# A hybrid attention/retention layer: merged rows reloaded in place by thirds, first rows of x kept on chip, weights loaded in quarters, and a scheduler that models the DMA queue

## The chip, the cores and the metric

The kernel runs on one core of one Trainium2 chip. The metric is the device time of one execution in microseconds (us). The core's engines run side by side, each through its own list of instructions: TensorE (PE) multiplies matrices, VectorE (DVE), ScalarE (ACT) and GpSimd (POOL) work elementwise, and SyncE (SP) issues all DMAs, among them the DMA transposes, in the order of its list.

## The reference, cut to what matters

One step of a single layer, for 1024 prompt rows and 32 sample rows (T = 1056), model width 1024, 8 heads:

```python
h   = RMSNorm(x)
z   = h @ w_in          # q/k/v of differential attention, q/k/v/gate of retention, two branch gates
o_a = DiffAttn(h)       # chunk-block-causal, two softmax maps per head: a = p0 - lam * p1
o_r = Retention(h)      # per-frame causal, decay, rotary, chunkwise-recurrent
x   = x + (sigmoid(g_a) * o_a + sigmoid(g_r) * o_r) @ w_o
x   = x + SwiGLU(RMSNorm(x))
x   = x + sigmoid(RMSNorm(x) @ w_ple_gate) * (p @ w_ple)
```

The new keys, values and retention states are outputs too.

## The kernel before

Every large matrix product is done as three fp16 products of high and low parts (mm3, L520; project, L860 to L862): for one step over 128 of the inner width there are three matmuls.

**The heads (0 to about 965 us).** The rows of x are normalised, transposed by PE (t, L834) and kept as xh (high and low part, 1056 rows). For each of 8 heads and 9 row blocks (eight of 128 rows, the ninth the sample) there is a unit A and a unit B. Unit A projects q, k, v and the retention q and k: 24 matmuls of 128x512 into a PSUM tile pj. Then come the scores sc (L1003 to L1006), the row maximum nm (DVE, L1013), its scaled negative nb (L1015), the exponential p (ACT, L1023), the difference of the two softmax maps and its split into fp16 parts (DVE), a DMA transpose aT<-p (SP, L1056), and the product po with v (L1064 to L1068). Unit B, which follows four units later (LAG), projects the retention v and the gates and computes the retention: a transposition on PE (pr, L1257), its copy qT (L435), pr and por (L1270 to L1273), the mask inn (DVE, L1276), por again (L1278). The merged result ms of a unit is transposed by DMA to mixT (L1357) and stored to DRAM (mix_d, by the helper store, L423 to L432, so that its line is L427). q and kT reach their layout by DMA transposes too (L1193, L1195).

Weights come as blocks of 1 MB (load_block_steps, L439): a stage buffer st is filled, an absolute maximum or a sum of squares gives a scale, and the block is split into fp16 parts. The very first blocks come as four quarters of 256 KB, each with its own DMA (due == 0, L449 on), the others in one DMA (L454).

**w_o.** When a head's blocks are in mix_d, last_mix (L1455 on) loads the merged rows back as mixs, by row ranges of 352 and by high and low part (L1463). mixs is a new tile of the pool of xh, allocated after the last projection. wo_rows multiplies the first 352 rows (block 0) by w_o, with the matching rows of x loaded as xr (L1417), adds, and stores them to x1_d. For the other blocks (1 of 352 rows, 2 and 3 of 176) w_o follows in the next stage; residual(0) reads block 0 back from x1_d (L1706) and scales it for the feed-forward.

**The rest (from about 998 us).** Residuals and norms of the four blocks (L1687 sums of squares, L1719 to L1728 scaling on DVE), the gate and up products as seven Strassen-like products over combined inputs (tT, x parts; parts are combined on DVE at L1595 on, weights at L549 to L558), the down projection, and the gated embedding at the end.

**What sets the order.** Each piece of work is a Python generator. A list scheduler (class Flow, L112) simulates the engines M (PE), V, S, G and D (the DMA issues): every step names an engine and a cost, the earliest possible one is taken, and instructions are emitted in that order. PE, DVE, ACT and POOL run their lists in exactly that order. Buffers are counted (get and put), events order the rest (wait and set). SP's list is written in the order in which the DMAs are emitted. Costs are plain functions: V, S, G for the elementwise engines, DM(mb) for a load (2.9 us per MB), X(us) and xbar(tiles) for stores and transposes, and fixed delays for the landing.

Of the kernel before, what the change touches and what calls it, by code (L numbers as in the profile page):

```python
# [11 lines left out]
F32 = mybir.dt.float32  # L12
# [9 lines left out]
P = 128  # L22
# [5 lines left out]
NT = 9  # L28
# [15 lines left out]
LAG = 4  # L44
NQ = 6
# [41 lines left out]
def DM(mb):  # L87
    return {"D": mb * 2.9}


def X(us):
    return {"D": us}


def xbar(tiles):

    return 1.15 + 0.006 * tiles


def landed(tiles):  # L100

    return ("delay", 1.3 + 0.02 * tiles)
# [9 lines left out]
class Flow:  # L112
    def __init__(self, buffers, shared=False):
        self.shared = shared
        self.free = {e: 0.0 for e in "MVSGD"}
        self.port = {"V": 0.0, "G": 0.0}
        self.buffers = {k: [0.0] * n for k, n in buffers.items()}
# [4 lines left out]
    def add(self, gen, prio=0, at=None):  # L122
        self.n += 1
        self._step([gen, prio, self.n, self.now if at is None else at, None, False], None)

    def _step(self, c, value):

        while True:
# [43 lines left out]
            elif kind == "delay":  # L172
                c[3] += key
            elif kind == "wait":
# [5 lines left out]
    def run(self):  # L180
        while self.ready:
# [12 lines left out]
            if isinstance(us, Own):  # L194
                self.port[e] = start + us
            c[3] = start + us + (0.0 if e == "M" else LAT)
# [19 lines left out]
def kernel(  # L216
# [63 lines left out]
    acc0 = const.tile([P, CH], F32, name="acc0")  # L280

# [43 lines left out]
    def weight_scale(amax, n, gi, tag, pool=True, norm=False, total=False, at_bank=None):  # L325
# [29 lines left out]
        d = sm(n, tag + "d", 6)  # L355
# [67 lines left out]
    def store(out, in_, key, us, event=None):  # L423

        yield ("delay", us)
        yield X(0.5)
# [3 lines left out]
        if key:  # L430
            yield ("delay", 2.5)
            yield ("put", key)  # L432
# [6 lines left out]
    def load_block_steps(src, w, b, gi, tag, rowf, out, tail=False, due=None, late=None, hold=None):  # L439
# [4 lines left out]
        if due == 0:  # L444
# [6 lines left out]
            yield ("set", "wl%d" % b)  # L451
        else:
            yield DM(1.0)
            nc.sync.dma_start(out=st, in_=src)  # L454
            yield ("delay", 3.0)
# [105 lines left out]
    def load_gu(j):  # L561

        yield ("get", "st")
        st = stage()[:, 0:KD * 256].rearrange("p (k u c) -> p k u c", k=KD, u=2)
        yield DM(1.0)
        nc.sync.dma_start(out=st, in_=wgu[j])
        yield ("delay", 2.0)
# [40 lines left out]
        yield ("put", "st")  # L608


    with ExitStack() as pa:
# [3 lines left out]
        id16 = ca.tile([P, P], F16, name="id16")  # L615
# [50 lines left out]
        def const_a():  # L666
# [3 lines left out]
            yield ("delay", 2.0)  # L670
# [14 lines left out]
        def const_c():  # L685
# [3 lines left out]
            yield ("delay", 2.0)  # L689
            yield ("set", "id")  # L690
            yield ("wait", ("x", 0))
            yield V(P)
            nc.vector.tensor_copy(id16, id32)

        def const_g():
# [3 lines left out]
            yield ("delay", 2.0)  # L699
# [12 lines left out]
        def const_b():  # L712
# [11 lines left out]
            yield ("delay", 2.0)  # L724
# [69 lines left out]
        def norm_x(i):  # L794
# [15 lines left out]
            yield ("delay", 3.0)  # L810
# [80 lines left out]
        def rms_small(ss, R, n, tag):  # L891

            yield GP(0, 0.5 + 0.2 * n)
# [5 lines left out]
        def prep_head_a(h, w, e):  # L899
# [8 lines left out]
            yield X(0.5)  # L908
            nc.sync.dma_start(out=s0[0:64], in_=st0[h])
            gr = hp.tile([P, P], F32, tag="grn", name="grn", bufs=2)  # L910
            yield X(0.5)
# [9 lines left out]
        def cache_steps(h, dA, e):  # L921
# [5 lines left out]
            for dst, src in ((kc[0:64], ckT[h]), (kc[64:128], ckT[h]), (vc, cv[h])):  # L927
                yield X(0.9)
                nc.sync.dma_start(out=dst, in_=src)
            yield ("delay", 4.0)  # L930
# [61 lines left out]
        def attend(key, i, R, q4, sblocks, masked, vblocks, NK, sc_ap, do_ap):  # L992
# [3 lines left out]
            for ms in ((0, 1),) if NK <= 512 else ((0,), (1,)):  # L996
# [19 lines left out]
                for m in ms:  # L1016
                    yield ("get", "p")
                    yield S(NK, 0.14)
# [36 lines left out]
            yield X(xbar(2 * nb_ * R // 16))  # L1055
# [1146 lines left out]
```

## Time and profile before

| What | us |
|---|---|
| Median of three runs | 1839.96 (1838.93 to 1841.03) |
| The profiled execution | 1841.03 |
| Its span | 1839.2 |
| PE busy | 1791.3 |
| DVE busy | 1456.2 |
| ACT busy | 1064.7 |
| POOL busy | 613.6 |

The profile is of one execution. A row of its timeline holds start, length, engine, line of the kernel, operation, output<-inputs by the program's names, and in brackets the idle time before it and what ended that. A row of its list of waits gives who waited for whom, the total, the number of times and the longest. A row of its DMA list gives the size of one DMA in KB and the median time from issue to landing.

### The profile page before, as it was taken

What the parts mean: (1) busy time and instruction counts of PE and PEld (TensorE: products, weight loads), DVE (VectorE), ACT (ScalarE), POOL (GpSimd) and SP (SyncE); (2) the same over time, 40 slices, a digit from 0 to 9 for tenths busy, and PEclk for the clock granted to TensorE, in tenths of its full rate; (3) what the DMA queues carried; (4) which work ended last, traced back from release to release, by engine and by line L of the source; (5) the groups of instructions that cost most, each with busy time, mean ns of one, the idle gap of its engine ahead of it and who ended that gap; (6) DMA issues with size and microseconds to landing.
All of it is one profiled execution on the core that took longest, in us unless ns stands there. A gap on an engine that the chain in (4) does not pass through costs nothing.

```text
span 1839.2 us, 37083 instructions
## 1 busy us (share of the span) xinstructions
PE 1791.3 (97%) x13391; PEld 1153.4 (63%) x13391; DVE 1456.2 (79%) x3883; ACT 1064.7 (58%) x2750; POOL 613.6 (33%) x1036
## 2 busy tenths in 40 slices
PE   7899999999999999999989999999999999999999
PEld 3455555555555555555556867777777766666666
DVE  7888788788787887888885889999999967544553
ACT  7677777677777777777654445655556522102421
POOL 3554546454554555545530002323232100000110
PEclk9999999999999999999999999999999999999999
DMA  6344434345443543435367203221211163221111
GB/s 202 106 124 110 111 82 100 99 107 125 87 116 91 119 111 83 123 80 126 84 151 252 78 5 105 82 93 59 70 47 63 40 264 107 67 78 47 51 48 44
DMA packets 235563, 180.98 MB, mean 98 GB/s; under 512 B 187345, under 2 KB 217553, under 8 KB 227186
## 3 DMA queue, kind: packets, MB, share of 16 engines
q1 hardware_dynamic: 235378, 178.61, 34.6%
q8 instruction: 105, 1.72, 0.4%
q14 instruction: 80, 0.66, 0.1%
HBM read 112.34 MB, written 27.02 MB: 76 GB/s over the span
## 4 chain that ended last, share of the span: by engine, by line
PE 82%; DVE 10%; DMA 3%; ACT 2%; issue 2%; POOL 2%; SPq 0%; POOLq 0%; ACTq 0%; DVEq 0%
PE pj L860 10%; PE pj L861 10%; PE pj L862 9%; PE ps L521 9%; PE ps L522 9%; PE ps L523 9%; PE ps L1571 4%; PE ps L1570 4%; PE ps L1569 4%; DMA aT<-p 2%; PE sc L1003 2%; PE sc L1006 2%; PE pj L871 1%; PE po L1064 1%; PE po L1068 1%
## 5 line engine op out<-in xcount | busy, mean ns | idle before, releaser
L860 PE MATMUL pj<-w,xh 128*128 128x512 f16 x1024 | 389.9, 381 | 3.1 <-ACT w L512 1.7
L861 PE MATMUL pj<-w,xh 128*128 128x512 f16 x1024 | 390.0, 381 | 0.8 <-DVE w L514 0.8
L862 PE MATMUL pj<-w,xh 128*128 128x512 f16 x1024 | 389.9, 381 | 0.0
L521 PE MATMUL ps<-mixs,w 128*128 128x176 f16 (+1 forms) x864 | 231.2, 273 | 2.0 <-DVE xr L1432 1.7
L523 PE MATMUL ps<-mixs,w 128*128 128x176 f16 (+1 forms) x864 | 231.3, 273 | 1.4 <-DVE w L549 1.4
L522 PE MATMUL ps<-mixs,w 128*128 128x176 f16 (+1 forms) x864 | 231.2, 273 | 0.9 <-DVE mixs L1595 0.9
L523 PEld LDWEIGHTS <-w 128*128 128x128 f16 x1632 | 160.0, 98 | 53.8 <-issue 5.4
L522 PEld LDWEIGHTS <-w 128*128 128x128 f16 x1632 | 160.0, 98 | 48.5 <-issue 2.1
L521 PEld LDWEIGHTS <-w 128*128 128x128 f16 x1632 | 160.2, 98 | 48.2 <-issue 0.9
L862 PEld LDWEIGHTS <-xh 128*128 128x128 f16 x1024 | 100.4, 98 | 123.2 <-issue 3.2
L860 PEld LDWEIGHTS <-xh 128*128 128x128 f16 x1024 | 101.0, 99 | 89.2 <-issue 2.2
L861 PEld LDWEIGHTS <-xh 128*128 128x128 f16 x1024 | 100.4, 98 | 85.2 <-issue 3.7
L558 POOL TENSOR_TENSOR st<-st 128x512 f32<-128x512 f32 x54 | 71.8, 1330 | 237.6 <-DVE w L549 182.6
L522 PE MATMUL ps<-tT,w 128*128 128x352 f16 (+1 forms) x504 | 137.3, 277 | 3.2 <-DVE tT L1595 3.2
L523 PE MATMUL ps<-tT,w 128*128 128x352 f16 (+1 forms) x504 | 137.3, 277 | 0.0
L521 PE MATMUL ps<-tT,w 128*128 128x352 f16 (+1 forms) x504 | 137.3, 277 | 0.0
L1023 ACT ACTIVATE p<-sc,nb,scs 128x256 f32<-128x256 f32 (+7 forms) x128 | 106.2, 831 | 51.1 <-DVE nb L1015 37.9
L549 DVE SCALAR_TENSOR_TENSOR w<-st,gus,w 128x512 f16<-128x512 f32 x126 | 128.4, 1022 | 0.0
L1013 DVE TENSOR_REDUCE nm<-sc 128x1 f32<-128x640 f32 (+6 forms) x112 | 102.7, 917 | 23.0 <-PE sc L1006 22.0
L1571 PE MATMUL ps<-a,w 128*128 128x352 f16 x312 | 97.5, 313 | 0.5 <-DVE w L1776 0.5
L1570 PE MATMUL ps<-a,w 128*128 128x352 f16 x312 | 97.5, 313 | 0.0
L1569 PE MATMUL ps<-a,w 128*128 128x352 f16 x312 | 97.5, 312 | 0.0
(442 smaller groups left out, 4707.5 us busy)
## 6 DMA issues: line engine op xcount, KB each, us to landing
st<-in_win_dram SPq DMA_DIRECT2D x30, 1024.0 KB, 5.3
st<-in_wgu_dram SPq DMA_DIRECT2D x22, 1024.0 KB, 4.9
st<-in_wdn_dram SPq DMA_DIRECT2D x16, 704.0 KB, 4.1
out_dram<-kv SPq DMA_DIRECT2D x64, 128.0 KB, 1.9
a_d<-a SPq DMA_DIRECT2D x9, 528.0 KB, 2.7
b<-a_d SPq DMA_DIRECT2D x9, 528.0 KB, 7.1
mixs<-mix_d SPq DMA_DIRECT2D x6, 704.0 KB, 7.2
x<-x_d SPq DMA_DIRECT2D x8, 528.0 KB, 7.7
```

The lines of the kernel that those rows point to most:

```text
L521: nc.tensor.matmul(out=ps, lhsT=wh, rhs=ah, start=first, stop=False)
L522: nc.tensor.matmul(out=ps, lhsT=wh, rhs=al, start=False, stop=False)
L523: nc.tensor.matmul(out=ps, lhsT=wl, rhs=ah, start=False, stop=last)
L549: nc.vector.scalar_tensor_tensor(out=w[:, i, 1], in0=src, scalar=s, in1=w[:, i, 0], op0=ALU.mult, op1=ALU.subtract)
L860: nc.tensor.matmul(out=ps, lhsT=xhi, rhs=w[:, k, 0], start=(k == 0), stop=False)
L861: nc.tensor.matmul(out=ps, lhsT=xhi, rhs=w[:, k, 1], start=False, stop=False)
L862: nc.tensor.matmul(out=ps, lhsT=xh[:, k, 1, t0:t0 + P], rhs=w[:, k, 0], start=False, stop=(k == KD - 1))
L1013: nc.vector.tensor_reduce(out=nm[0:R, mc], in_=pv, axis=AX.X, op=ALU.max, negate=True)
L1023: nc.scalar.activation(pt[0:R, 0:NK], ps[0:R, p0:p0 + NK], AF.Exp, bias=nb[0:R, m:m + 1], scale=sc_ap[0:R], accum_out=Z[0:R, m:m + 1])
L1569: nc.tensor.matmul(out=ps, lhsT=wt[:, 0, j], rhs=a[:, 0, cs], start=(first and j == js[0]), stop=False)
L1570: nc.tensor.matmul(out=ps, lhsT=wt[:, 1, j], rhs=a[:, 0, cs], start=False, stop=False)
L1571: nc.tensor.matmul(out=ps, lhsT=wt[:, 2, j], rhs=a[:, 1, cs], start=False, stop=(last and j == js[-1]))
```

## The change

Merged rows. They are now loaded into xh itself. last_mix starts when the last head begins its fifth block; each third waits until the last head's B projections no longer read its rows (event free), and then is loaded (L1484 of the new file). The first product with w_o waits for the first third through the event mc, 5.5 us in the scheduler's time.

Block 0. xrow_load loads the first 352 rows of x before their use, six of the eight row groups into a weight stage buffer (st) and two into a tile of their own, x67. wo_rows adds into them, they stay there, and residual(0) and the combinations read them in place; the reload from x1_d is gone, the store to it stays. The stage buffer is given back by rows_free; until then the next stage has one stage buffer, and the second gate/up load has a tile of its own, sx.

Weights. Every block loaded by load_block_steps comes as four DMAs of 256 KB.

Scheduler. A DMA step now carries its size. Flow keeps a time at which the queue is free, adds the size by 0.26 MB per us (0.2 for a transpose), and lets landed() wait for that time. Some costs are changed, and the projection order is written as a string (ORDER) that begins with four A units, as the lag did. The transposed-merge buffers are 3 instead of 4, and an unused fp16 identity goes.

```diff
-def DM(mb):
-    return {"D": mb * 2.9}
-
-
-def X(us):
-    return {"D": us}
+class Dma(float):
+    mb, turn = 0.0, False
+
+
+def DM(mb, turn=False):
+    d = Dma(1.15 + 1.5 * mb if turn else 0.4)
+    d.mb, d.turn = mb, turn
+    return {"D": d}
...
+            if isinstance(us, Dma):
+                self.queue = max(self.queue, start + (0.9 if us.turn else 0.5)) + us.mb / (0.2 if us.turn else 0.26)
+                c[6] = max(c[6], self.queue + (1.3 if us.turn else 1.05))
+                c[3] = start + us
...
-            yield DM(1.0)
-            nc.sync.dma_start(out=st, in_=src)
-            yield ("delay", 3.0)
+            for q in range(4):
+                yield DM(0.25)
+                nc.sync.dma_start(out=st[:, 2 * q:2 * q + 2], in_=src[:, 2 * q:2 * q + 2])
+            yield landed()
...
-                    yield S(NK, 0.14)
+                    yield S(NK, 0.24)
...
+        def xrow_load():
+
+            yield ("get", "st")
+            st = stage()[:, 0:6 * CH].rearrange("p (k t) -> p k t", k=6)
+            for k in range(0, 6, 2):
+                yield DM(0.36)
+                nc.sync.dma_start(out=st[:, k:k + 2], in_=xT[:, k:k + 2, 0:CH])
+            yield DM(0.36)
+            nc.sync.dma_start(out=x67, in_=xT[:, 6:8, 0:CH])
+            yield landed()
+            tail["x1"] = lambda ks: st[:, ks] if ks.start < 6 else x67[:, ks.start - 6:ks.stop - 6]
+            yield ("set", "xr")
...
             for n, (cs, top) in enumerate(((slice(0, CH), 3), (slice(CH, 2 * CH), 6), (slice(2 * CH, T), NT))):
+                yield ("wait", ("free", top - 1))
...
-                if (h, i) == (H - 1, NT - 1):
-                    tail["mixs"] = xh_pool.tile([P, KD, 2, T], F16, tag="xh", name="mixs")
-                        flow.add(last_mix(), 0)
+                    if h + 1 == H:
+                        yield ("set", ("free", i))
...
-                else:
-                    nc.sync.dma_start(out=xf, in_=x1_d[:, :, cs].rearrange("k p t -> p k t"))
-                    yield ("delay", 7.0)
```

PE issues the same products in another order; SP's list grows from 592 to 616 rows. Three places follow, with rows as they stand in the two lists.

First, PE at the first attention of the program: sc are a unit's scores (kT times q, mneg and mrow the mask), t the transposition of an input tile, po the product with v. Before:

```order
L1064 MATMUL po<-vh,aT 128x128
L1065 LDWEIGHTS aT
L1065 MATMUL po<-vh,aT 128x128
L1068 LDWEIGHTS aT
L1068 MATMUL po<-vh,aT 128x128
L834 MATMUL t<-cst_sb,w 128x32 x4
L860 LDWEIGHTS xh
L860 MATMUL pj<-w,xh 128x512
```

The first unit's scores stand 100 rows ahead of this, with input tiles and projections between. In the changed kernel the rows from the first unit's last scores to its po are these; q_731 is the first unit's, q_816 the second's:

```order
L1017 MATMUL sc<-kT,q_731 128x128
L845 MATMUL t<-cst_sb,w 128x32 x4
...
L1017 MATMUL sc<-kT,q_816 128x256
L1268 MATMUL pr<-cst_sb,qk 128x128
L1281 MATMUL pr<-qz_136,qT 128x128
L1284 MATMUL pr<-vr,qk 128x128
L1075 LDWEIGHTS aT
L1075 MATMUL po<-vh,aT 128x128
```

All input tiles are transposed ahead of this place now, and the scores of two units and the start of a retention stand between the first scores and po.

Second, PE at the end of the heads, from the last rows of the last attention unit to the first product with w_o. Before (mt belongs to the scales of w_o):

```order
L1068 MATMUL po<-vh,aT 128x128
L1278 MATMUL por<-vr,inn 128x128
L311 MATMUL mt<-cst_sb,wam 1x128 x2
L322 MATMUL mt<-o0mc,cst_sb 128x1
L322 MATMUL mt<-o1mc,cst_sb 128x1
L1257 MATMUL pr<-cst_sb,qk 128x128
L1270 MATMUL pr<-qz_137,qT 128x128
L1272 MATMUL por<-s_142,qz_137 128x128
L1273 MATMUL pr<-vr,qk 128x128
L521 LDWEIGHTS w
L521 MATMUL pj<-mixs,w 128x352
```

And in the changed kernel:

```order
L1079 MATMUL po<-vh,aT 128x128
L1268 MATMUL pr<-cst_sb,qk 128x128
L898 MATMUL pj<-cst_sb,suz 128x128 x4
L1281 MATMUL pr<-qz_136,qT 128x128
L1283 MATMUL por<-S_140,qz_136 128x128
L1284 MATMUL pr<-vr,qk 128x128
L1268 MATMUL pr<-cst_sb,qk 128x128
L1289 MATMUL por<-vr,inn 128x128
L1281 MATMUL pr<-qz_137,qT 128x128
L1283 MATMUL por<-s_142,qz_137 128x128
L1284 MATMUL pr<-vr,qk 128x128
L1289 MATMUL por<-vr,inn 128x128
```

The scales of w_o have moved ahead of the last gate tiles, and two retention units stand back to back behind the last po; the first product with w_o follows the last row.

Third, SP around the transposes of the last full unit (128x16x128) and of the sample unit (the 128x10x128 behind it). Before:

```order
L1056 DMA_TRANSPOSE aT<-p 128x14x128
...
L1056 DMA_TRANSPOSE aT<-p 128x16x128
L454 DMA st<-in_wo_dram 128x2048
L1357 DMA_TRANSPOSE mixT<-ms 128x2x128
L1417 DMA xr<-in_xT_dram 128x2x352 x2
L427 DMA mix_d<-mixT 256x1x128
L1056 DMA_TRANSPOSE aT<-p 128x10x128
L1463 DMA mixs<-mix_d 128x8x352 x3
```

In the changed kernel:

```order
L1067 DMA_TRANSPOSE aT<-p 128x14x128
L1484 DMA xh<-mix_d 128x8x352 x2
...
L467 DMA st<-in_wo_dram 128x512 x2
L1204 DMA_TRANSPOSE q_15178<-qst 128x2x128
L467 DMA st<-in_wo_dram 128x512
L1206 DMA_TRANSPOSE kT<-qst 128x4x32
L467 DMA st<-in_wo_dram 128x512
L1067 DMA_TRANSPOSE aT<-p 128x16x128
...
L1067 DMA_TRANSPOSE aT<-p 128x10x128
L1484 DMA xh<-mix_d 128x8x352 x2
```

The first third of the merged rows and the last block of w_o, now in quarters, are issued ahead of the last full unit's transpose instead of behind it.

More of the change, by code (lines that the diff above doesn't have):

```diff
@@ L44 @@
 LAG = 4
+ORDER = "AAAA"
 NQ = 6
@@ L116, in __init__ @@
         self.port = {"V": 0.0, "G": 0.0}
+        self.queue = 0.0
         self.buffers = {k: [0.0] * n for k, n in buffers.items()}
@@ L123, in add @@
         self.n += 1
-        self._step([gen, prio, self.n, self.now if at is None else at, None, False], None)
+        self._step([gen, prio, self.n, self.now if at is None else at, None, False, 0.0], None)
     def _step(self, c, value):
@@ L280 @@
     acc0 = const.tile([P, CH], F32, name="acc0")
+    x67 = const.tile([P, 2, CH], F32, name="x67")
     ones16 = ones32.bitcast(BF16).rearrange("p (c t) -> p c t", t=2)[:, :, 1]
@@ L1423, in wo_rows @@
             mixs = tail["mixs"]
+            xr = tail["x1"](slice(m, m + 2))
             for n in range(2):
@@ L1463, in last_mix, with loaded @@
                     nc.sync.dma_start(out=tail["mixs"][:, :, a, cs], in_=mix_d[:, :, a, cs].rearrange("h p t -> p h t"))
-                    if n == 0:
-                        flow.add(mark(("mc", a), 2.0))
-        def mark(key, us):
-            yield ("delay", us)
-            yield ("set", key)
+                if n == 0:
+                    flow.add(loaded(), 0)
+        def loaded():
+            yield ("delay", 5.5)
+            for a in range(2):
+                yield ("set", ("mc", a))
         def stream():
+            tail["mixs"] = xh
             env, wAs, wBs = {}, {0: []}, {}
@@ L1505, in stream @@
                     if i == 4 and h + 1 == H:
+                        flow.add(last_mix(), 0)
                         flow.add(load_wo(0, (0, 1)), 1)
@@ L1585 @@
             xfs, dns, banks = {}, {}, {}
+            x1 = tail["x1"]
             def span(c):
@@ L1695, in root, with rows_free @@
                 return ps, r
+            def rows_free():
+                for k in range(HK):
+                    yield ("wait", ("o", 1, "t2", k))
+                    yield ("wait", ("o", 0, "t4", k))
+                yield ("put", "st")
             def residual(c):
@@ L1701, in residual, with rows @@
                 cs = span(c)
-                xf = xc.tile([P, KD, CW], F32, tag="xf%d" % p, name="xf", bufs=2)
                 if c:
+                    xf = xc.tile([P, KD, CW], F32, tag="xf%d" % p, name="xf", bufs=1 + p)
+                    yield DM(CW / 250.0)
                     nc.sync.dma_start(out=xf, in_=xT[:, :, cs])
-                else:
-                    nc.sync.dma_start(out=xf, in_=x1_d[:, :, cs].rearrange("k p t -> p k t"))
-                    yield ("delay", 7.0)
-                xfs[c] = xf
+                    xfs[c] = xf
+                def rows(ks):
+                    return xf[:, ks] if c else x1(ks)
                 n = ROWS[p]
                 B = CW // 4
-                yield ("get", "acc")
-                if not c:
+                if c:
+                    yield ("get", "acc")
+                else:
                     yield ("wait", ("wo", 1, 0))
                     ps, r = yield from root(0, acc0)
-                else:
+                if c:
                     ps, r = yield from row_norm(c, xf)
@@ L1734, in residual @@
                         ks = slice(k, k + n)
-                        flow.add(parts16((p, "x1" if k < HK else "x3", k % HK), (xh1[:, ks, 0, cs], xh1[:, ks, 1, cs]), xf[:, ks]))
+                        flow.add(parts16((p, "x1" if k < HK else "x3", k % HK), (xh1[:, ks, 0, cs], xh1[:, ks, 1, cs]), rows(ks)))
                     elif k >= HK:
```

122 lines of the change are left out of this document (64 added, 58 removed).

## The prediction

> **What bounds the kernel now.** I read the page first: one core, and TensorE (PE) busy for almost the whole span.
>
> ```profile
> span 1839.2 us, 37083 instructions
> PE 1791.3 (97%) x13391; PEld 1153.4 (63%) x13391; DVE 1456.2 (79%) x3883; ACT 1064.7 (58%) x2750; POOL 613.6 (33%) x1036
> ```
>
> The change leaves PE's products as they are, so it can only win or lose idle PE time, 1839.2 - 1791.3 = 47.9 us, and the time at a lower granted clock. The profiled execution took 1841.03 us, 1.83 above its span and 1.07 above the median 1839.96 of three runs. The sum below is a difference, made on the profiled execution and applied to the median. About 0.2%, 3.7 us, is what a measurement of this kernel can tell from no change.
>
> Next, the table of stretches (length; busy us of PE, weight loads, DVE, ACT and POOL, each with its instructions; granted clock; share of the DMA engines; GB/s) shows where the idle time lies.
>
> ```profile
> 0.00:40.00 40.00, 28.55 (x114) 13.82 (x115) 29.96 (x102) 30.77 (x63) 11.06 (x23) 1.00 0.67 223
> 40.00:80.00 40.00, 34.70 (x184) 18.40 (x183) 32.11 (x83) 25.54 (x74) 26.20 (x47) 0.91 0.41 116
> 80.00:120.00 40.00, 38.56 (x279) 21.15 (x278) 36.60 (x117) 32.94 (x91) 23.25 (x42) 1.00 0.44 121
> 120.00:160.00 40.00, 36.43 (x243) 20.32 (x242) 32.81 (x90) 29.28 (x79) 14.20 (x28) 1.00 0.41 86
> 160.00:860.00 700.00, 694.72 (x4964) 398.25 (x4963) 574.11 (x1806) 523.39 (x1545) 369.29 (x702) 1.00 0.43 104
> 950.00:970.00 20.00, 13.75 (x127) 10.64 (x127) 16.90 (x61) 10.77 (x37) 4.42 (x12) 0.74 0.85 214
> 1060.00:1120.00 60.00, 54.19 (x438) 38.36 (x436) 55.98 (x149) 29.05 (x63) 2.39 (x2) 0.97 0.12 38
> 1120.00:1800.00 680.00, 679.04 (x5399) 489.48 (x5398) 527.61 (x1086) 281.23 (x546) 113.80 (x99) 1.00 0.23 80
> ```
>
> Idle are 11.45 us in the first 40, 5.3 in the next, 5.0 from 80 to 160, 5.3 in the 700 us of the heads, 6.25 at the end of the heads, 5.8 after 1060, and hardly any from 1120 on. Last, PE's waits (total, times, longest) say on what:
>
> ```profile
> PE po L1064 <- DMA aT<-p: 11.4, 9, 4.5
> PE ps L522 <- DVE tT L1595: 3.2, 3, 1.6
> PE pj L887 <- DVE suz L884: 2.6, 1, 2.6
> PE ps L521 <- DVE xr L1432: 1.7, 1, 1.7
> PE pr L1257 <- DVE o0c L266: 1.6, 1, 1.6
> ```
>
> The largest is the attention's second product waiting for its transposed weights, on SP's queue. No wait in this list is for a weight load as such, or for the reloaded x1. So the edits to these loads act through where they stand among the transposes, and through the order that the list scheduler now writes.
>
> **The change, part by part.**
>
> *Quarters.* These DMA groups (KB of each, us from issue to landing) price them:
>
> ```profile
> st<-in_win_dram SPq DMA_DIRECT2D x30, 1024.0 KB, 5.3
> st<-in_win_dram SPq DMA_DIRECT2D x8, 256.0 KB, 5.2
> mixs<-mix_d SPq DMA_DIRECT2D x6, 704.0 KB, 7.2
> xf<-x_d SPq DMA_DIRECT2D x1, 1408.0 KB, 7.7
> aT<-p SPq DMA_TRANSPOSE x72, 3.2
> ```
>
> A whole block lands in 5.3 us; quarters, issued in a train, in 5.2 each. So a train saves no landing time; its gain is that a transpose may stand between quarters. The Trainium skill ("DMA: Bandwidth & Descriptors", section Bandwidth) speaks against this edit: it says to batch transfers to 1 MiB or more, and gives 78% of peak at 1 MB. The rows here do not show it, and at 0.43 DMA share the lost rate would be hidden; by it the sum would be no better than zero here. The new order still has four quarters of a block mostly in a row, and about as many transposes close behind a block as before. I price 160 to 860 at -1 us: of 5.3 idle, between -4 (nearly all gone) and +4 (as much again). SP issues three more DMAs per block, beside PE's work.
>
> *The start.* Here the new order differs most. Before, the first unit's scores stand well ahead of its po; now scores and po of units 0 and 1 stand close together, after five input tiles' and one gate tile's projections.
>
> ```profile
> 47.47 0.22 PE L1003 MATMUL sc<-kT,q 128*128 128x128 f16 x1
> 60.39 0.60 PE L834 MATMUL t<-cst_sb,w 128*128 128x128 f32 x4
> 65.52 0.29 PE L1064 MATMUL po<-vh,aT 128*128 128x128 f16 x1 [4.53 <-DMA aT<-p]
> 69.21 0.40 PE L1006 MATMUL sc<-kT,q 128*128 128x256 f16 x1
> 394.76 0.22 PE L1006 MATMUL sc<-kT,q 128*128 128x128 f16 x1
> 404.52 0.23 PE L1064 MATMUL po<-vh,aT 128*128 128x128 f16 x1
> ```
>
> Counted in products, PE reaches the first scores of the new order about where it stood before at 60.39 plus 0.6, near 61. Before, scores to po took 18.1 us, on a DVE busy with input tiles; a later first unit needed 9.8 without a wait. With 9.8, po is at 70.8; as much PE work had been done before when the second unit's scores ended, at 69.6. That is +1.2; with the full 18.1 it is +9.5. The input tiles are done by then, so the 9.8 row is nearer. Unit 1's transpose follows on the same queue with only 3.5 us of products behind its scores, +1 to +2. Against it stand the 5.0 us idle from 80 to 160, of which a pipeline that fills later and more evenly should keep some off: I take -1.5 of them. In all +1.5, between -1 and +8. The early load of 0.36 MB for two of the rows of x (x67) stands ahead of the second weight block on SP, by at most one landing of a block, 5.3 us; the first scores wait for DVE's input tiles rather than for that block: nothing, at most +1.
>
> *The end of the heads.* Rows of the tail (the first two give the pace, 0.22 us from one 512-column product to the next):
>
> ```profile
> 928.05 0.38 PE L861 MATMUL pj<-w,xh 128*128 128x512 f16 x1
> 928.27 0.38 PE L862 MATMUL pj<-w,xh 128*128 128x512 f16 x1
> 932.64 0.38 PE L1006 MATMUL sc<-kT,q 128*128 128x512 f16 x1
> 942.63 1.89 SPq L1056 DMA_TRANSPOSE aT<-p  x1
> 948.50 0.22 PE L1064 MATMUL po<-vh,aT 128*128 128x128 f16 x1
> 956.20 0.66 DVE L473 TENSOR_REDUCE wam<-st 128x2 f32<-128x512 f32 x1
> 956.33 1.11 PE L887 MATMUL pj<-cst_sb,suz 128*128 128x128 f32 x4 [2.56 <-DVE suz L884]
> 962.39 0.35 PE L1257 MATMUL pr<-cst_sb,qk 128*128 128x128 f32 x1 [1.65 <-DVE o0c L266]
> 964.43 0.80 PE L1270 MATMUL pr<-qz,qT 128*128 128x128 f32 x2 [1.69 <-ACT qT L435]
> 965.87 0.50 PE L521 MATMUL pj<-mixs,w 128*128 128x352 f16 x1
> ```
>
> Here the eight absolute maxima of the last two w_o blocks, 0.66 us each on DVE like the one shown, stand among the rows that suz waits for, and PE's row behind it waits for the scales of w_o (o0c): 2.56 + 1.65 = 4.2 us, and another 1.69 for qT. Now maxima and scales come before the last gate tiles, which removes the 4.2. What is late next: the last two retention units stand back to back with no projection between them and w_o's first product, so qT and two masked products are bare, where one qT was: +1.5 (0 to +4). And the last full unit's po stands 9.0 us of products behind its scores (15 before). Before, its transpose was issued 10.0 us after them and takes 3.2 to land, 13.2 in all; so PE waits between 0, if the DVE queue is shorter now, and 4.2; I take 1.7. The first third of the merged rows and a w_o block in quarters stand on SP ahead of that transpose, at most 7.2 us of landing if they block it; they are issued some rows earlier, so that I add nothing. Sum -4.2 + 1.5 + 1.7 = -1, between -6 and +5. The thirds themselves free nothing else: w_o's first product started at 965.87, 1.4 us behind the row at 964.43, with two retention products between, and waited for no load.
>
> *Rows that stay on chip.* The reload of x1 (7.7 us) had no one waiting on PE's list; the new loads to a stage buffer are as large as those they replace. Zero, up to +1 if the stage buffer comes back late to the gate/up weights; those have their own tile for product 1. The wait of 1.7 us at xr stays: it is the hand-over of PSUM.
>
> *After 1060.* DVE is what PE waits for.
>
> ```profile
> 1060.00:1072.00 12.00, 8.81 (x66) 5.27 (x64) 12.00 (x31) 5.16 (x12) 0.00 (x0) 0.99 0.03 9
> 1037.44 1.40 DVE L549 SCALAR_TENSOR_TENSOR wx<-st,gus,wx 128x512 f16<-128x512 f32 x2
> ```
>
> In the new order such a pair of weight products, a single one and a weight subtraction, 1.4 + 0.7 + 0.7 = about 2.8 us, stand ahead of block 1's scaling instead of between it and the tT rows. But the norm of block 1, from which these rows come, is 24 narrow products later: at the 679.04/5399 = 0.126 us of a product of the stretch from 1120 to 1800 at most 3.0 us, for narrow ones near 1.8. Left is -1 (-4 to +2) of the 3.2 us that PE waited for tT.
>
> **Sum**: -1 + 1.5 - 1 + 0 - 1 = -1.5 us, 1839.96 - 1.5 = about 1838.5.
>
> **The rivals.** *The start opens a hole (slower).* If the chain from scores to transpose takes 14 us instead of 9.8 because the first units queue together on DVE and SP, po is at 75 and unit 1's behind it; from about 12 us on it decides, since nothing else on PE is ready. Price +6 to +8 at the start, total 1846. For it: 1.4 us of products between scores and po. Against: the input norms are done. *The end of the heads closes up (faster).* From 950 to 970 PE was idle 6.25 us and had a mean clock of 0.74; were both gone, with the 20 - 6.25 = 13.75 us of work done at 1.00, that is 6.25 + 0.26 x 13.75, near 9.8 us; allowing 2 us for the bare qT, -8: 1830. *Clock.* The rows
>
> ```profile
> 60.00:65.00 5.00, 0.99 (x7) 0.56 (x5) 4.62 (x13) 1.45 (x4) 2.10 (x3) 0.99 0.98 253
> 65.00:70.00 5.00, 4.48 (x22) 2.49 (x23) 2.77 (x11) 3.46 (x14) 2.32 (x5) 0.50 0.53 119
> ```
>
> show that 4 us idle in one five were followed by a clock of 0.50 in the next, in which 4.48 us of PE time did half their products: 2.2 us. If the last full unit's wait reaches 4.2 us and the start's hole is one piece, two such stretches are added: +4.4 on top of a sum near zero, 1844. The Trainium skill ("TensorE: Matmul & The Clock Gate", section on what is happening) has the clock halve after an idle window of some 3.4 us and return after as long a busy one; the trace agrees with 4.53 us idle and half clock behind it. *Nothing moves.* The loads were hidden and the order is as good as the old: 1840.
>
> **Chances.** Forecast 0.4, over about -6 to +4 (0.12 of it faster, 0.25 the same, 0.03 slower); tail closes up 0.2; hole at the start 0.2; clock 0.1; nothing moves 0.1 (0.07 same, 0.03 faster). So faster 0.35, same 0.32, slower 0.33. The range takes in the tail's case and the hole: 1828 to 1849; the likeliest case's own is 1834 to 1844.
>
> **What would show it.** Right: po's first wait at the start is 6 to 10 us and those between 80 and 160 shrink; the waits on suz and o0c are gone; po of the last full unit waits below 3 us; the idle time from 1060 to 1072 falls to about 2. Wrong: a wait on aT above 10 us at the start, more than ten waits of po on aT among the heads, a wait for the merged rows at w_o's first product, or a new wait on gate/up weights.

## The result and the profile after

The changed kernel took 1852.45 us, the median of four runs (1850.32 to 1853.61), beside 1840.49 for the kernel before (1838.93 to 1844.19): a ratio of 1.0055, 95% interval 1.0041 to 1.0069. It is slower by about 10 us (8 to 13 by the interval), and 1852 lies above the range predicted, 1828 to 1849. Measured a second time, later, the ratio was 1.0035 (1.0022 to 1.0047). By that ratio the time would be about 1846, inside the range but above the likeliest case's own, 1834 to 1844; slower it is in both. The profiled execution took 1852.38 us with a span of 1850.6.

The page's head, to be laid beside the one of before:

```profile
span 1850.6 us, 37313 instructions
PE 1793.0 (97%) x13391; PEld 1153.7 (62%) x13391; DVE 1455.3 (79%) x3894; ACT 1054.1 (57%) x2735; POOL 612.9 (33%) x1039
```

PE does the same 13391 products in the same time (1793.0 against 1791.3). Its idle time went from 47.9 to 57.6 us. The same stretches, with the same columns as in the prediction:

```profile
0.00:40.00 40.00, 28.12 (x119) 14.66 (x120) 29.46 (x98) 29.03 (x58) 8.35 (x24) 1.00 0.71 233
40.00:80.00 40.00, 30.49 (x162) 16.83 (x160) 36.92 (x105) 28.57 (x81) 27.66 (x48) 0.83 0.42 112
80.00:160.00 80.00, 79.43 (x539) 44.14 (x538) 63.94 (x184) 57.83 (x165) 38.01 (x72) 1.00 0.46 101
160.00:860.00 700.00, 684.04 (x4829) 388.95 (x4827) 561.85 (x1770) 505.55 (x1493) 360.38 (x684) 1.00 0.47 102
860.00:950.00 90.00, 89.34 (x653) 51.92 (x651) 78.82 (x251) 63.09 (x199) 46.07 (x89) 1.00 0.49 108
950.00:1010.00 60.00, 52.46 (x382) 34.07 (x380) 44.80 (x131) 27.90 (x73) 11.42 (x22) 0.91 0.66 189
1060.00:1120.00 60.00, 54.98 (x544) 44.03 (x542) 57.66 (x153) 29.57 (x69) 3.17 (x2) 1.00 0.12 40
1120.00:1800.00 680.00, 678.07 (x5392) 488.64 (x5390) 531.97 (x1103) 284.83 (x551) 112.43 (x96) 1.00 0.24 81
```

Two rows of before that the prediction did not show:

```profile
860.00:950.00 90.00, 87.68 (x595) 50.19 (x593) 75.03 (x226) 57.12 (x172) 44.46 (x81) 1.00 0.38 95
950.00:1010.00 60.00, 52.02 (x388) 35.86 (x388) 39.27 (x112) 25.94 (x66) 4.98 (x12) 0.91 0.86 252
```

A stretch's work is its PE time multiplied by its clock. Up to 160 us that is 28.55 + 0.91 x 34.70 + 75.00 = 135.1 before and 28.12 + 0.83 x 30.49 + 79.43 = 132.9 now: 2.2 us behind. (The product is rough where idle time and half clock fall into one stretch; with the time at half clock counted on its own it is 1.7.) In the 700 us of the heads it is 694.72 against 684.04: another 10.7 us. And the rounded clock of 1.00 hides one piece of these 700 us that ran at half clock, which costs 1.7 more:

```profile
812.66:816.07 3.41, 1.48 (x23) 1.26 (x22) 0.35 (x1) 0.65 (x4) 0.00 (x0) 1.00 0.81 191
816.07:819.48 3.41, 3.41 (x13) 1.65 (x12) 1.25 (x2) 2.85 (x11) 0.84 (x3) 0.50 0.11 24
```

So the heads are 12.4 us behind, which is the whole loss and a little more. The other stretches nearly cancel: from 860 to 1010 it is 1.7 + 0.4 us ahead, from 1010 to 1060 0.7 behind (49.32 us of PE time against 50.00), from 1060 to 1120 2.4 ahead (0.97 x 54.19 against 54.98), from 1120 to 1800 1.0 behind (679.04 before). Together that is 11.8 us, where the spans differ by 11.4; the clock's rounding is enough for the rest. The idle time of the heads has trebled, from 5.3 to 16.0 us, and it is spread: PE's waits in that stretch, first of before, then of after (total, times, longest).

```profile
PE po L1064 <- DMA aT<-p: 4.7, 5, 1.8
PE sc L1003 <- DMA kT<-qst: 0.3, 1, 0.3
```

```profile
PE po L1075 <- DMA aT<-p: 10.0, 9, 2.2
PE sc L1014 <- DMA kT<-qst: 4.0, 4, 1.7
```

Nothing takes more than 2.2 us at once; there are simply nine late transposes aT where there were five, and four late kT. They come late in two ways. The longest shows the first. SP's list there, and PE's row that waited:

```profile
431.00 1.96 SPq L467 DMA_DIRECT2D st<-in_win_dram  x4
433.05 1.17 SPq L1368 DMA_TRANSPOSE mixT<-ms  x1
436.95 0.57 SPq L438 DMA_DIRECT2D mix_d<-mixT  x1
437.61 1.30 SPq L1067 DMA_TRANSPOSE aT<-p  x1
...
442.21 0.23 PE L1075 MATMUL po<-vh,aT 128*128 128x128 f16 x1 [2.22 <-DMA aT<-p]
```

The last DVE operation on p began at 433.8 and took 0.75 us. But the store of mixT stands ahead of aT's transpose in SP's list, and that store waited 2.6 us for mixT to land. So aT was issued 3 us after its data was ready, and PE, with too little other work listed in between, ran dry. No run moves the stores of mixT to another engine.

The second way, at the next longest:

```profile
806.04 1.55 SPq L467 DMA_DIRECT2D st<-in_win_dram  x3
807.69 2.13 SPq L1067 DMA_TRANSPOSE aT<-p  x1
...
814.81 0.23 PE L1075 MATMUL po<-vh,aT 128*128 128x128 f16 x1 [1.93 <-DMA aT<-p]
```

Here p was ready at 807.3 and aT was issued at once, directly behind a train of quarters. But it landed only 7.1 us after its issue; the median of the 55 in this stretch is 3.4. Four of the nine waits are of this kind, with landings of 4.2 to 7.1 us, and they make up 4.3 of the 10.0 us. How often the list brings this about can be counted: of the 55 transposes of aT between 160 and 860 us, 1 stood directly behind a load of weights in SP's list before, and 14 do now.

The start and the end of the heads in the changed kernel:

```profile
60.25 0.22 PE L1017 MATMUL sc<-kT,q 128*128 128x128 f16 x1
66.19 0.37 PE L1014 MATMUL sc<-kT,q 128*128 128x256 f16 x1 [5.36 <-DMA kT<-qst]
69.44 0.77 PE L1281 MATMUL pr<-qz,qT 128*128 128x128 f32 x2 [1.92 <-DVE qT L446]
70.42 0.31 PE L1075 MATMUL po<-vh,aT 128*128 128x128 f16 x1
...
956.14 0.18 PE L1014 MATMUL sc<-kT,q 128*128 128x32 f16 x1 [2.83 <-DMA kT<-qst]
980.33 0.80 PE L1289 MATMUL por<-vr,inn 128*128 128x128 f32 x2 [0.96 <-DVE inn L1287]
```

The first po runs at 70.4 without a wait of its own. The hole stands ahead of it, at the second unit's scores, which wait for that unit's kT.

### The profile page after: what moved, and what is told of

Same layout as the page of the kernel before. It is cut to its first block, busy times and chain, and to the rows that moved or that the text cites. A ratio compares the mean times of both kernels' runs of the same rounds, so it can differ in the third digit from the quotient of the medians.

```text
span 1850.6 us, 37313 instructions
## 1 busy us (share of the span) xinstructions
PE 1793.0 (97%) x13391; PEld 1153.7 (62%) x13391; DVE 1455.3 (79%) x3894; ACT 1054.1 (57%) x2735; POOL 612.9 (33%) x1039
## 4 chain that ended last, share of the span: by engine, by line
PE 82%; DVE 7%; DMA 5%; ACT 2%; issue 2%; POOL 1%; SPq 0%; POOLq 0%; ACTq 0%; DVEq 0%
PE pj L871 10%; PE pj L872 10%; PE pj L873 10%; PE ps L534 9%; PE ps L535 9%; PE ps L536 9%; PE ps L1597 4%; PE ps L1595 4%; PE ps L1596 4%; DMA aT<-p 3%; PE sc L1014 2%; PE sc L1017 2%; DMA kT<-qst 1%; PE po L1075 1%; DVE w L562 1%
## 5 line engine op out<-in xcount | busy, mean ns | idle before, releaser
L535 PE MATMUL ps<-xh,w 128*128 128x352 f16 (+1 forms) x1000 | 272.3, 277 | 1.8 <-DVE xh L1623 1.8
L534 PE MATMUL ps<-xh,w 128*128 128x352 f16 (+1 forms) x1000 | 272.4, 277 | 0.7 <-DVE x L1453 0.7
L536 PE MATMUL ps<-xh,w 128*128 128x352 f16 (+1 forms) x1000 | 272.4, 277 | 0.0
```

The lines of the kernel that those rows point to most:

```text
L534: nc.tensor.matmul(out=ps, lhsT=wh, rhs=ah, start=first, stop=False)
L535: nc.tensor.matmul(out=ps, lhsT=wh, rhs=al, start=False, stop=False)
L536: nc.tensor.matmul(out=ps, lhsT=wl, rhs=ah, start=False, stop=last)
```

## The experiments

Ratios are to the kernel before, with 95% intervals; 0.001 is 1.84 us. The theories: A, the loss is that of the split loads; B, it is that of the new DMA times in the scheduler, through the order that it writes; C, any newly written order loses. Later ones are stated with their experiment. Idle times are PE's in the profiled execution, 160 to 860 us, against 5.3 before and 16.0 in the changed kernel.

### Is it the split loads?

**The changed kernel with whole loads, all five orders kept.** The first quarter's DMA carries the block, the other three are not issued.

```diff
-                nc.sync.dma_start(out=st[:, 2 * q:2 * q + 2], in_=src[:, 2 * q:2 * q + 2])
+                if not q:
+                    nc.sync.dma_start(out=st, in_=src)
```

> The changed kernel with each later 1 MB weight block loaded by one DMA, issued where the first of its four quarters stood; every engine but SP keeps its list. Theory A (the quarters, as DMAs among the transposes, make q, kT and aT late): most of the 14 us lost between 400 and 870 comes back, 1841 to 1845, and the waits of scores on kT fall from 12 us to below 6. Theory B (the scheduler's new landing times write a PE order with too little work ahead of each transposed operand): no change within 2 us, 1850 to 1854, the waits stay.

Measured: 1848.37, 1.0037 (1.0023 to 1.0051). That is no less than the second measurement of the changed kernel, 1.0035, and 3 us below its first, 1.0055. The heads' idle time stays:

```profile
160.00:860.00 700.00, 685.86 (x4849) 391.32 (x4848) 564.93 (x1779) 507.83 (x1499) 362.98 (x688) 1.00 0.44 103
```

14.1 us without a single split load behind the first blocks. A explains at most some 2 to 3 us. Nine transposes of aT still stand directly behind a load here; the one that landed in 7.1 us behind its train of quarters now follows a whole block and a store, and lands in 6.1 us.

**The kernel before with quarters, its orders kept.**

```diff
-            nc.sync.dma_start(out=st, in_=src)
+            for q in range(4):
+                nc.sync.dma_start(out=st[:, 2 * q:2 * q + 2], in_=src[:, 2 * q:2 * q + 2])
```

> The kernel before with each 1 MB block as four quarters in a row at the same place; every engine but SP keeps its list. Theory A: slower than before by 4 to 12 us, with longer waits on aT and kT. Theory B: within 2 us of before, 1839 to 1842.

Measured: 1850.24, 1.0043 (1.003 to 1.0055). So in the old order quarters cost 8 us. The waits of this kernel and two of its DMA groups (the latter with the median from issue to landing):

```profile
PE po L1065 <- DMA aT<-p: 19.1, 13, 4.9
```

```profile
st<-in_win_dram SPq DMA_DIRECT2D x128, 256.0 KB, 4.0
aT<-p SPq DMA_TRANSPOSE x72, 3.3
```

Waits on aT went from 11.4 to 19.1 us, though a transpose still lands 3.3 us after its issue (3.2 before). By the median they are issued later, not slower. (This profiled execution is 5 us above the kernel's median, so its waits are rather too long.)

**The kernel before with halves.** The same edit with two DMAs.

> The kernel before with each 1 MB block as two halves in a row, all lists but SP's unchanged; four quarters cost 8 us there. Issue theory (each added DMA holds SP's list some 0.45 us ahead of a transpose): a third of the added DMAs, so +2 to +4, 1844 to 1846. Size theory (pieces below a block move slower as such): +4 to +8. Threshold theory (only a long train reaches the slack of the transposes): 0 to +1.5.

Measured: 1851.47, 1.0045 (1.003 to 1.006). Halves cost as much as quarters, so the loss is not proportional to the number of DMAs. One place comes back in several heads: SP before, then with halves.

```profile
453.50 0.37 SPq L454 DMA_DIRECT2D st<-in_win_dram  x1
453.98 1.18 SPq L1357 DMA_TRANSPOSE mixT<-ms  x1
455.25 1.19 SPq L1193 DMA_TRANSPOSE q<-qst  x1
456.54 1.22 SPq L1195 DMA_TRANSPOSE kT<-qst  x1
```

```profile
455.21 0.38 SPq L455 DMA_DIRECT2D st<-in_win_dram  x1
455.68 1.18 SPq L1358 DMA_TRANSPOSE mixT<-ms  x1
456.92 0.56 SPq L455 DMA_DIRECT2D st<-in_win_dram  x1
457.58 1.18 SPq L1194 DMA_TRANSPOSE q<-qst  x1
458.85 2.37 SPq L1196 DMA_TRANSPOSE kT<-qst  x1
...
463.64 0.39 PE L1004 MATMUL sc<-kT,q 128*128 128x512 f16 x1 [1.22 <-DMA q<-qst]
```

The second half stands between the transposes of mixT and q. So q is issued 2.37 us after the block's first DMA instead of 1.75, and kT's issue behind it takes 2.37 us instead of 1.22. PE, which waited nowhere for q before, waits 1.22 us. It does so four times in all, 3.7 us together.

**The kernel before with three loads of one number per partition beside each block**, 102 in all, of which nothing is read. This loads more than the program needs and leaves nothing out.

```diff
             nc.sync.dma_start(out=st, in_=src)
+            for q in range(3 if len(tiny) > 1 and tiny[1] < 102 else 0):
+                c = tiny[1]
+                tiny[1] += 1
+                nc.sync.dma_start(out=tiny[0][:, c:c + 1], in_=src[:, 2 * q, 0:1])
```

> The kernel before with whole loads and beside each three loads of one number per partition that nobody reads: as many added DMAs on SP's list as quarters add, with no split. If the cost of splitting is the added issues alone: 5 to 9 us slower than before, like quarters. If it is that the data come in pieces with transposes between them: within 2 us of before.

Measured: 1864.38, 1.012 (1.0106 to 1.0133); PE's wait on aT is

```profile
PE po L1070 <- DMA aT<-p: 25.1, 15, 3.6
```

Added issues on SP are enough, with blocks whole and some 50 KB more moved in all. This doesn't price quarters: 22 us is far above their 8, and with these loads aT also lands later, 3.6 us after its issue. Most of it is lost at the start: up to 160 us the work done is 116.6 us instead of 135.1, and only 6.6 of the 25.1 us of waits lie among the heads.

**The kernel before with the stores of keys and values issued by POOL**, `(nc.gpsimd if key == "kv" else nc.sync).dma_start(out=out, in_=in_)`. If a store that waits on SP holds up transposes, taking it away should win.

> The kernel before with the stores of new keys and values issued by POOL, which computes them, instead of SP. If SP's list, held by a store that waits for POOL (105 us in 35 waits), makes the transposes behind it late: PE's waits for aT fall from 11.4 us to below 6 and the time by 3 to 8 us, 1832 to 1838. If the transposes are late for another reason: 1838 to 1843; slower if issuing costs POOL more than 1 us each.

Measured: 1842.82, 1.0006 (0.9997 to 1.0015). Waits on aT fell from 11.4 to 6.7 us, those of the input tiles' t rose from 3.9 to 7.0. No time was won: waits on transposes are not a sum that can be taken back one by one.

### Is it the new DMA times, and the order they write?

**The changed kernel with the old costs of DMAs**, with quarters:

```diff
-    d = Dma(1.15 + 1.5 * mb if turn else 0.4)
+    d = Dma(1.15 + 1.5 * mb if turn else max(0.5, 2.9 * mb))
...
-                self.queue = max(self.queue, start + (0.9 if us.turn else 0.5)) + us.mb / (0.2 if us.turn else 0.26)
-                c[6] = max(c[6], self.queue + (1.3 if us.turn else 1.05))
+                c[6] = start + us + (1.1 + 5.12 * us.mb if us.turn else 2.8)
```

> The changed kernel with the scheduler's old costs and landing delays for DMAs (2.9 us per MB at the issuing engine, 1.3 us and 0.02 per tile for a transpose, 2.8 us for a load), quarters, thirds and rows on chip kept. Theory A: as slow as the changed kernel, 1849 to 1855, since the quarters stay. Theory B: the order has its slack back, 1840 to 1845, and idle PE time from 160 to 860 falls from 16 us to 5 to 8.

Measured: 1872.96, 1.0173 (1.0157 to 1.0189). **The same with whole loads** (one step of 1 MB for the four):

> The changed kernel with old scheduler times and whole 1 MB loads: what is left of the change is thirds, rows on chip and small constants. Both theories: about 1838 to 1842, near the kernel before. If it stays above 1848, neither theory holds and the thirds or the constants are the cause.

Measured: 1870.86, 1.016 (1.0145 to 1.0175). Both are about 20 us slower than the changed kernel, where B wanted them faster. In this program the new times help; B seemed refuted.

**The kernel before with the other changed costs alone**: `S(NK, 0.24)` for 0.14, `S(P, 0.1)` for 0.0 twice, `GP(0, 0.75 + 0.15 * n)` for `0.5 + 0.2 * n`.

> The kernel before with the changed scheduler's three cost constants alone (exponential 0.24 instead of 0.14 us over its length, small squares 0.1 more, root 0.75 + 0.15 n instead of 0.5 + 0.2 n); DMA times, loads and the rest as before. Theory C (any new list order of the heads loses, because the old order happened to leave the transposes enough slack): 5 to 25 us slower than before, idle PE time among the heads up from 5 us. Theory D (the constants are harmless, the loss is in thirds and rows on chip): 1838 to 1844.

Measured: 1842.08, 0.999 (0.9981 to 1.0). A newly written order that costs nothing: C falls as a rule. Yet in its profiled execution, 4 us above its median, the heads are idle for 9.1 us, and 7 transposes of aT stand directly behind a load; so neither figure alone fixes the time.

**The changed kernel with whole loads, approximately the old DMA times, and the old constants** (the edits above together), so that only the merged rows and the kept rows seemed to be left:

> The changed kernel with whole loads, the old DMA times and the old constants: thirds, rows on chip and the buffers that go with them are what is left. Theory C: the heads lie within 5 us of before, since their order is nearly the old one; the total 1836 to 1846. Theory D: 1855 to 1875, like the run with old DMA times and new constants.

Measured: 1873.69, 1.0165 (1.015 to 1.018). Its longest wait, 12.5 us, is at the gate/up scales (mt on wamh).

**The changed kernel with whole loads and the old constants, new DMA times:**

> The changed kernel with whole loads and the old constants, but the new DMA times: between the run with whole loads and new constants (1848) and that with thirds and rows alone. If the new DMA times are what costs: 1848 to 1856. If the constants are: 1838 to 1844.

Measured: 1863.22, 1.0107 (1.0092 to 1.0122). The constants, worth nothing in the kernel before, are worth 13 us between this kernel (1.0107) and the first experiment (1.0037). Such effects do not add up, so the next kernels hold the order itself still.

**The kernel before with the merged rows by thirds and the kept rows, costs and DMA times as before**, so that the heads keep their old order on PE, DVE, ACT and POOL. The edit is those parts of the change's diff, last_mix, xrow_load and wo_rows among them.

> The kernel before with thirds, rows on chip and their buffers alone: old DMA times, old constants, whole loads, and on PE, DVE, ACT and POOL the very list of before up to the end of the heads. Theory D (thirds and rows cost by themselves): 6 us slower or more, most of it from 930 to 1010 and at the start, where the two early rows of x now stand ahead of weights. Theory E (they are harmless or help; the loss of the changed kernel is the new order of the heads and the split loads): 1836 to 1842, heads as before.

Measured: 1844.94, 1.0016 (1.0008 to 1.0025).

```profile
160.00:860.00 700.00, 693.21 (x4957) 397.21 (x4956) 572.64 (x1801) 522.82 (x1544) 367.62 (x700) 1.00 0.46 104
```

This is the kernel that the one at 1873.69 was meant to be. By name the same pieces, they are 27 us apart by their ratios. They differ in small numbers of the scheduler, in the loop that orders the projections and in the copy of the unused identity; which of these writes the worse order, no run shows. These two parts of the change cost 3 us, and the heads' idle time is 6.8.

**The kernel before with the new DMA times in its scheduler alone** (the class Dma, the queue and landed() of the change's diff). The loads are whole, but the scheduler counts each as four steps of 0.25 MB, as the changed kernel does; the first step's DMA carries the block:

> The kernel before with the new DMA times in the scheduler alone: whole loads, old constants, merged rows and x as before. If the new times write a worse order of the heads: 4 to 10 us slower than before, mostly at the start (two scores close together) and among the heads. If they are harmless: within 2 us of before, and the changed kernel's loss is split loads plus thirds and rows (8 + 3 us).

Measured: 1859.65, 1.0094 (1.0079 to 1.0109): 17 us slower, more than was expected.

```profile
40.00:80.00 40.00, 27.46 (x136) 14.44 (x134) 32.75 (x87) 26.13 (x73) 25.04 (x45) 0.78 0.44 107
...
160.00:860.00 700.00, 688.77 (x4858) 390.96 (x4857) 571.02 (x1798) 507.40 (x1500) 352.68 (x689) 1.00 0.42 103
```

Of the edits to the kernel before, this one opens a hole at the start like the changed kernel's: 12.5 us idle from 40 to 80 at a clock of 0.78, where the changed kernel has 9.5 at 0.83. (Here PE waits for ACT's p, 6.9 us, and not for kT.) In the heads it has 11.2 us idle. B stands again, in a narrower form: not that new times are bad, but that a list written anew has its own price.

**The same with quarters**, PE's list unchanged:

> The same with the loads in quarters; PE's list is that of the run with the new times alone, word for word. If the split costs as it does in the old order: 6 to 9 us over that run. If the new order, which knows of the queue, makes room for quarters: 0 to 4 us over it.

Measured: 1861.33, 1.01 (1.0082 to 1.0118): the intervals overlap almost wholly, the heads' idle time is 13.8 us. In an order written for four quarters, splitting costs 1.7 us by the medians, which cannot be told from nothing (each interval is some 3 us to either side); in the old order it cost 8 us.

**The changed kernel again**, unchanged:

> The changed kernel again, on the chip and beside the runs of the other three: 1849 to 1854. Its ratio to before is what the sum of the parts is held against.

Measured: 1849.76, 1.0035 (1.0022 to 1.0047), heads' idle time:

```profile
160.00:860.00 700.00, 682.93 (x4835) 388.81 (x4833) 563.16 (x1772) 506.42 (x1494) 359.89 (x683) 1.00 0.47 102
```

17.1 us: the loss in the heads repeats, though the whole came out less slow.

### The early load, and room for the transposes

**The load of x67 held back** by `nc.gpsimd.memset(x67[:, :, 0:1], 0.0)` ahead of it, first in the kernel with the old order of the heads:

> The same with the load of the two rows of x that have a tile of their own held back to the end of the heads by a small memset of that tile, so that it no longer stands among the first weight loads. If that early load costs: 2 to 5 us faster than the run without it, with the wait of po at the start back to 4.5 us. If not: equal within 1.5 us.

Measured: 1846.74, 1.0025 (1.0015 to 1.0035), no better than 1.0016 without. In the changed kernel:

> The changed kernel with that load held back in the same way, all else as in it. If the early load makes the hole at the start (idle 8.9 us from 60 to 80): 2 to 5 us faster, 1847 to 1850. If the list order makes it: 1851 to 1854 and the wait of 5.4 us on kT stays.

Measured: 1848.28, 1.0034 (1.0022 to 1.0046), the same as the changed kernel's repeat. The wait for kT at the start is 3.90 us, against 5.36 in the first profile and 3.96 in the repeat's. The early load is not the cause.

**More room for transposes.** If the scheduler counts on landings that come too soon, it should do better with later ones. In the changed kernel, 1 us more for a transpose to land:

```diff
-                c[6] = max(c[6], self.queue + (1.3 if us.turn else 1.05))
+                c[6] = max(c[6], self.queue + (2.3 if us.turn else 1.05))
```

> The changed kernel with one change in the scheduler's numbers: it takes a DMA transpose to land 1 us later, so that it writes more other work on PE between a transpose and its use (on average 15.1 us of products between scores and po, instead of 13.9; 14.4 before). If too little slack for the transposes is what costs: waits of PE on aT and kT among the heads fall from 10 us and more to below 6, and the time by 3 to 8 us. If not: within 3 us of the changed kernel, or worse.

Measured: 1861.47, 1.0112 (1.0095 to 1.0128). PE's waits from 160 to 860:

```profile
PE pj L871 <- DVE gu L1329: 10.5, 4, 4.9
PE mt L347 <- DVE wamh L493: 3.3, 2, 1.8
PE sc L1014 <- DMA kT<-qst: 1.1, 3, 0.8
PE po L1075 <- DMA aT<-p: 0.7, 2, 0.5
```

The waits on aT and kT went from 14.0 to 1.8 us, as foreseen, and PE waits 13.8 us for gu and the weight scales instead: idle time of 16.1 us, as in the changed kernel. **With 2 us more** (3.3):

> The same with 2 us (16.0 us of products on average). If slack is what costs: the waits on aT and kT among the heads fall further, below 3 us; the time is then set by the start, the end of the heads and whatever the longer distance delays, 1838 to 1848. If not: no fewer waits than with 1 us.

Measured: 1866.59, 1.0133 (1.0118 to 1.0148), slower still, with 7.0 us of waits for the weight scales (mt on wamh) and again 6.1 us for aT.

Short landing times explain the waits on transposes, not the time: taking these waits away made the list worse elsewhere.

## Why the prediction was wrong, point by point

**Quarters, 160 to 860: -1, between -4 and +4. This is the step that failed.** It priced the heads by the loads alone: three more issues per block, about as many transposes close behind a block as before. It gave the newly written order of the heads no price of its own. Measured: 10.7 us of idle time and 1.7 at half clock. The order brings most of this, not the split: with whole loads in the changed order 14.1 us of idle time stay, with the new DMA times alone there are 11.2, with the old heads order and these two parts, thirds and rows, 6.8. The premise of as many transposes close behind a block could have been counted in the two lists. All kinds together, 19 stand directly behind a load of weights before and 24 after, so it nearly held; but those of aT, which po waits for, went from 1 to 14. The counts for aT go with the idle time in the kernels above (1 and 5.3 us, 1 and 6.8 with the old heads order, 9 and 14.1 with whole loads, 14 and 16.0), but no run changes them alone, so that part of the cause is argued. The prediction had named the sign itself, more than ten waits of po on aT among the heads; there were nine, and four on kT, and in the repeat twelve. The bound of "as much again" was no bound: 5.3 us idle out of 700 is what was left by a list that happens to fit well, and nothing in the trace of before kept a new list from leaving three times as much.

The Trainium skill ("DMA: Bandwidth & Descriptors", section Bandwidth) would have quarters slower by their size, and the Trainium skill ("Perfetto Trace Analysis", section DMA Optimizations) says that splitting may let some chunks start sooner. Neither decided here: in the old order a quarter landed in 4.0 us where a block took 5.3, PE's wait for a split weight stayed at 1.7 us, and the waits that grew were those on the transposes behind the loads on SP (on aT from 11.4 to 19.1 us, of 8 us lost).

**The start: +1.5, between -1 and +8.** Measured 2.2 by the work done up to 160 us; in the repeat, 27.68 + 0.87 x 31.11 + 79.43 = 134.2, about 0.9. (With the time at half clock counted on its own these are 1.7 and 0.1.) The size was right and the place wrong:

```profile
0.00:40.00 40.00, 27.68 (x119) 14.46 (x120) 29.59 (x98) 29.01 (x58) 7.89 (x22) 1.00 0.71 233
40.00:80.00 40.00, 31.11 (x171) 17.08 (x170) 37.76 (x106) 30.12 (x85) 29.23 (x51) 0.87 0.41 113
80.00:160.00 80.00, 79.43 (x540) 44.27 (x539) 64.91 (x188) 57.95 (x165) 37.76 (x72) 1.00 0.47 102
```

po stands at 70.4, predicted 70.8; but PE waited 5.36 us for the second unit's kT, not for aT. The stalls from 80 to 160 fell from 5.0 to 0.6 us, three times the 1.5 that were taken off, and the clock took some of it back. That the two errors cancel is luck:

```profile
65.00:70.00 5.00, 1.89 (x10) 1.36 (x10) 3.72 (x14) 4.27 (x16) 2.09 (x4) 0.51 0.35 80
```

That is the prediction's clock rival in one place: 5.36 us idle, then half clock. The Trainium skill ("TensorE: Matmul & The Clock Gate", section on what is happening) puts the halving after an idle window of some 3.4 us, and the trace agrees here. It does not at 816 us, in the two rows shown with the result: there the half clock followed 3.41 us in which PE was busy for 1.48, and its one wait was 1.93 us. So a wait well below 3.4 us can bring the half clock too. The early load of x67 costs nothing, as said.

**The end of the heads: -1, between -6 and +5.** From 950 to 1010 the work is 0.4 us more than before by the rounded clock, and 0.2 less with the time at half clock counted on its own: within its bounds. The waits on suz and o0c are gone, and qT and inn are bare, as foreseen: 1.1 us on qT and 1.9 on inn, 3.0 in all where +1.5 (0 to +4) was taken. The last full unit's po did not wait; the sample's scores did, 2.83 us for kT, whose transpose stands between quarters of w_o on SP. The term that was to cost 1.7 cost 2.8, at another transpose of the same list.

**Rows on chip: 0.** Right for the kept rows: the stage buffer was not waited for, and two waits on the scales of the gate/up weights come to 1.3 us. One part was wrong: the 1.7 us at xr became 0.7. With the thirds, and in the old order, these parts cost 3 us, most of it in the heads (idle 6.8 against 5.3) and behind 1120.

**After 1060: -1, between -4 and +2.** From 1060 to 1120 it was 0.8 us of idle time and 1.6 of clock (0.97 to 1.00), 2.4 in all. Within its bounds. PE's three waits for tT, 3.2 us, became one of 1.2, but two others came, 1.9 us on a residual xf and 1.8 on xh. The sign named for it can't be read off, since the same piece of work lies some 10 us later now.

**The rivals.** The hole at the start came, at the scores instead of po, and was given back before 160; the end of the heads did not close. The rival that was missing is the one that happened: many small waits, because the list written anew for the whole of the heads fits worse.

**What stays open.** Which of the new numbers makes the heads' order worse, and whether by its own error or because every cost in the scheduler was right only beside the others, no run tells. Nor does a run take the transposes out from behind the loads and leave the rest of the list as it is. Lists that differ in such numbers came out between 1842 and 1874 us; none was faster than the kernel before by what can be measured (0.999, 0.9981 to 1.0, at best). The whole change is also better than its new DMA times alone (1.0035 to 1.0055 against 1.0094), and the runs do not say which part mends what.

## What to carry to other kernels

When a change touches what a list scheduler counts with, the new list has a price of its own over its whole length. Bound it by what other lists of the same program lose, here 30 us, not by the idle time that the present list happens to leave. Count in both lists what the prediction takes to be equal, here the transposes directly behind a load, each kind by itself. To test one part of such a change, hold the lists still and change that part alone; and judge a cost model by the time of the program, since one that removes a wait can bring a larger one elsewhere.

## What the runs showed of the hardware

A quarter of a 1 MB load landed 4.0 us after its own issue, a whole one 5.3, and splitting still cost 8 us in an order made for whole loads, as much in halves as in quarters. 102 loads of 512 bytes cost 22 us. The transposes of aT landed 3.3 us after their issue with quarters, 3.0 with halves and 3.6 beside the small loads, against 3.2, all medians; so by the median the cost with halves and quarters is the place in SP's list, where a plain issue took 0.4 to 0.6 us, a transpose 1.2, and a store that waits holds back all that stands behind it. A transpose issued directly behind the loads could also land late: 4.2 to 7.1 us in the four waits of the changed kernel, against a median of 3.4. And the clock was halved for 3.4 us after a stretch of the same length in which PE was idle for 1.93 us and busy for the rest.
